# A hybrid decoder step: keys, values and queries by seven block products on pairs of column tiles, with two tensors parked in DRAM

## The chip, the core and the metric

The kernel runs on one core of one Trainium2 chip. The core has a matrix engine (TensorE, in the profile PE, with its weight loads as PEld), a vector engine (VectorE, DVE), a scalar engine (ScalarE, ACT), a third engine for simple element work (GpSimd, POOL) and a sequencer (SyncE, SP) that here only issues DMA transfers. Each engine works through its own list of instructions in order and waits on semaphores. Sixteen DMA engines move data between DRAM and the on-chip memory (SBUF, 128 partitions). Matmul results go to banks of PSUM, an accumulating memory. The metric is the device time of one execution in microseconds (us); lower is better.

## The reference

One layer of a hybrid decoder is computed for 512 prompt tokens and 8 x 4 sample tokens with a width of 2048. One input projection feeds two groups of heads: gated linear attention (GLA), and sparse attention with a compressed branch, a selected branch and a window branch, each with its own keys and values. The parts that matter here:

```python
xn = rmsnorm(h, attn_norm_g[i])
proj = xn @ w_in[i]
gq, gk, gv, gr, ga, nq, kc, vc, ks, vs, kw, vw, ng = jnp.split(proj, offsets, axis=-1)
...
o_gla = rmsnorm(o_gla, gla_norm_g[i]).reshape(B, L, GLA_WIDTH).astype(x.dtype)
o_gla = o_gla * jax.nn.silu(gr)
o_nsa, nsa_new = nsa_mixer(nq, kc, vc, ks, vs, kw, vw, ng, ...)
h = h + jnp.concatenate([o_gla, o_nsa], axis=-1) @ w_out[i]
```

After it come a gated feed-forward part with a short convolution, a per-layer input term and a final norm. `kc` and `vc` (256 columns each) are the keys and values that are compressed; `ks`, `vs`, `kw`, `vw` (256 each) are those of the selected and window branches; `nq` are 8 query heads of 128 columns.

## The kernel before

**Layout.** Everything is kept with features on partitions and tokens along the free dimension. The 544 tokens are two groups `g` of 272 (256 prompt, 16 sample). The 2048 input features are 16 k-tiles. A column tile of `w_in` is 128 output columns. `xn` holds for each k-tile a high and a low part (`xh`, `xl`) of the input times its norm's gain, in the rounded type fp32r; the row scale `R1` is multiplied in after the product.

**One column tile.** `weights` (L155) loads two halves of the tile (512 KB each, 8 k-tiles) through SP into one of three `raw` buffers; ACT casts it to `wh` (L166) and DVE subtracts to get `wl` (L167), three buffers each. `product` (L171) then runs for each of 16 k-tiles three passes (`wh` by `xh`, `wh` by `xl`, `wl` by `xh`) for both token groups: 96 matmuls of 128 x 128 by 272 columns into a two-bank PSUM tile `mp`. DVE evicts with one multiplication by `R1`.

**Order of the stages.** A planner fixes the order of each engine's list when the program is built: it takes operations in the order in which the code states them, and lets a later one go ahead where an earlier one is not ready by its estimate. The stages are: tile 0 (gates), then four GLA heads `h` of 6 tiles each (L463 to L667). At the end of a head the gated outputs are split into high and low parts in `og{h}` (L662 to L665), in the pool `ogla`, and stay there as `o_gla`. Then the loop at L679 makes 12 tiles, two for each of `cmp_k`, `cmp_v`, `slc_k`, `slc_v`, `win_k`, `win_v`. Each is stored by SP (L696); the compression's tiles are reordered by POOL into the tokens `rp` (L699), and values are transposed by PE (L704). The loop at L714 makes 8 query tiles `nq`, which POOL also copies in part into `qs` (L723). Then `xn` is released, and the next stage starts: POOL loads the compression's weights (L353) and the residuals (L735), PE runs the first halves of the output products on `o_gla` (L737, `first_half`) and the compression of the prompt's tokens (`hidden`, L365). Later the attention reuses the `og` buffers for cached keys and values (L831).

**Seven products elsewhere.** The up projection (`up`, L1209) and the down projection (L1366) already multiply pairs with seven block products instead of eight. There `parts` (L1182) splits a half tile of weights and `multiply` (L1189) runs one block product: 8 k-tiles, three passes, one group of tokens, 24 matmuls.

Of the kernel before, what the change touches and what calls it, by code (L numbers as in the profile page):

```python
# [8 lines left out]
F32 = mybir.dt.float32  # L9
F32R = mybir.dt.float32r  # L10
# [93 lines left out]
def trunk(ctx, tc, I, O, stop=None, tap=None):  # L104
# [66 lines left out]
    def product(pp, ws, xs, groups=slice(0, G), ks=None):  # L171
        n = len(ws)
        for k in ks or range(n):
            (wh, wl), (xh, xl) = ws[k], xs[k]
            for w, x, first, last in ((wh, xh, k == 0, False), (wh, xl, False, False), (wl, xh, False, k == n - 1)):
                for g in range(G)[groups]:
                    mm = nc.tensor.matmul(pp[g][:, :GN] if isinstance(pp, list) else pp[:, g, :GN], w, x[:, g],  # L177
                                          start=first, stop=last)
        return mm
# [278 lines left out]
    def blk(t, b):  # L458
        return t[:, b // 2, (b % 2) * 128:(b % 2) * 128 + 128]

    o_gla = []
    ntile = 1
    for h in range(4):  # L463
        qk = []
# [192 lines left out]
        for dv in range(2):  # L657
            f = flat(oT[dv])
            nc.vector.scalar_tensor_tensor(f, f, v1("gn", dv), flat(rs), op0=ALU.mult, op1=ALU.mult)
            nc.vector.tensor_mul(oT[dv], oT[dv], sg[dv])  # L660
            if dv == 0:
                og = op_.tile([128, 2, 2, G, GN], F32R, tag=f"og{h}", name=f"og{h}")  # L662
            hi, lo = og[:, dv, 0], og[:, dv, 1]
            nc.scalar.copy(hi, oT[dv])
            nc.vector.tensor_sub(lo, oT[dv], hi.bitcast(F32))  # L665
# [10 lines left out]
    rp = {}  # L676
    vt = {}
    vn = {}
    for ty, name in enumerate(("cmp_k", "cmp_v", "slc_k", "slc_v", "win_k", "win_v")):  # L679
        keep = name in ("slc_k", "win_k")  # L680
        if name[:3] == "cmp":
            rp[name] = kp.tile([128, 4, 16, 2, 8], F32, name="rp_" + name)
        elif not keep:
            vt[name] = ap.tile([128, 4, 256], F32, name="vt_" + name)
            vn[name] = ap.tile([32, 256], F32, name="vn_" + name)
        for g in range(2):
            pp = main_ps()
            product(pp, weights(wsrc("w_in", ntile)), xn)
            ntile += 1
# [5 lines left out]
            nc.vector.tensor_mul(f, pp[:, :, :GN], R1)  # L695
            nc.sync.dma_start(O[name][g], f)  # L696
            if name[:3] == "cmp":
                for a in range(2):
                    nc.gpsimd.tensor_copy(rp[name][:, 2 * a:2 * a + 2, :, g].rearrange("p c j n -> p c n j"),  # L699
                                          f[:, a, :PN].rearrange("p (c n j) -> p c n j", n=8, j=16))  # L700
            elif not keep:
                s = side_ps()
                for b in range(4):
                    nc.tensor.transpose(s[:, b * 128:b * 128 + 128], blk(f, b), ident)  # L704
                nc.scalar.copy(vt[name][:, :, g * 128:g * 128 + 128], s.rearrange("p (b c) -> p b c", b=4))
                fs = kp.tile([128, 32], F32, tag="fs", bufs=2, name="fs")
# [4 lines left out]
    nq = []  # L711
    qs = ap.tile([128, 2, 8, 32], F32, name="qs")
    nc.gpsimd.memset(qs, 0.0)
    for h in range(8):  # L714
        pp = main_ps()
        product(pp, weights(wsrc("w_in", ntile)), xn)
        ntile += 1
        q = ap.tile([128, G, GN], F32, tag=f"nq{h}", name=f"nq{h}")
        nc.vector.scalar_tensor_tensor(q, pp[:, :, :GN], ATT_SCALE, R1, op0=ALU.mult, op1=ALU.mult)
        nq.append(q)  # L720
        r = h % 4
        for gr in range(2):
            nc.gpsimd.tensor_copy(qs[:, h // 4, 4 * gr:4 * gr + 4, 4 * r:4 * r + 4],  # L723
                                  q[:, gr, PN:].rearrange("p (b t) -> p b t", t=DS))
# [20 lines left out]


    cp, cp_s = pool("cmp", "left")
    ckp = ap.tile([128, 2, 32], F32, name="ckp")
    cvp = ap.tile([128, 2, 128], F32, name="cvp")
# [18 lines left out]
    kp_s.close()  # L768
    tap("ckp", ckp)
    tap("cvp", cvp)  # L770
    if stop == "cmp":
# [15 lines left out]

    attention_out(bp, range(4))
    lp, lp_s = pool("ple", "left")
    OS = ap.tile([128, 8, 32], F32, name="OS")  # L790
# [120 lines left out]
    def sample_step(i):  # L911
# [8 lines left out]
            s_a(*sunits[i])  # L920
        if i == len(sunits):
            tap("OS", OS)

    def split(hi, lo, src):
        nc.scalar.copy(hi, src)  # L925
        nc.vector.tensor_sub(lo, src, hi.bitcast(F32))  # L926

    pcTs = {}
    st = {}
# [176 lines left out]
    def split_scaled(hl, src, scale):  # L1106

        if scale is None:
            split(*hl, src)
            return  # L1110
        nc.scalar.activation(hl[0], src, AF.Copy, scale=scale)  # L1111
        nc.vector.scalar_tensor_tensor(hl[1], src, scale, hl[0].bitcast(F32), op0=ALU.mult, op1=ALU.subtract)

    def stemp(pl, bufs=4):
        return pl.tile([128, GN], F32, tag="st", bufs=bufs, name="st")

    def scaled(out, src, scale, other, op):
        nc.vector.scalar_tensor_tensor(out, src, scale, other, op0=ALU.mult, op1=op)

    first = True  # L1120
    for n in [k + h * HK for k in range(HK) for h in range(2)]:
# [54 lines left out]
    def set_size(name, ph):  # L1176
# [5 lines left out]
    def parts(raw, kn=8, neg=False):  # L1182
        wh = wp.tile([128, 8, 128], F32R, tag="wh", bufs=3, name="wh")
        wl = wp.tile([128, 8, 128], F32R, tag="wl", bufs=3, name="wl")
        w3 = [a[:, :kn].rearrange("p k n -> p (k n)") for a in (raw, wh, wl)]
        split_scaled(w3[1:], w3[0], -1.0 if neg else None)
        return wh, wl

    def multiply(ps, w, a, start, stop):  # L1189
        n = len(a)  # L1190
        for k in range(n):
            for i, (wi, xi) in enumerate(((0, 0), (0, 1), (1, 0))):
                nc.tensor.matmul(ps[:, :GN], w[wi][:, k], a[k][xi], start=start and k == 0 and i == 0,  # L1193
                                 stop=stop and k == n - 1 and i == 2, skip_group_check=True)

    def bank(tag):
        return st_.tile([128, 512], F32, tag=tag, bufs=2, name=tag)
# [458 lines left out]
```

## Time and profile before

| what | us |
|---|---|
| median of 3 timed runs | 2716.22 |
| lowest and highest of them | 2716.19 and 2719.57 |
| the profiled execution | 2723.27 |
| its span, first to last instruction | 2721.4 |
| ACT busy in it | 1150.4 |
| POOL busy in it | 446.1 |

The profile is of one execution. Its page gives each engine's busy time, forty slices of the span, the chain of work that ended last, and groups of equal instructions. The trace behind it answers further views: instructions in order of time (start, duration, engine, line, what is written and read, and in brackets the idle time before and what ended it; an "x2" behind a line says that two instructions are merged in it), tables by stretches of time, who waited for whom, and DMA issues with their time to landing. Matmuls are pipelined: the duration of one is longer than the distance between two starts.

### The profile page before, as it was taken

What the parts mean: (1) busy time and instruction counts of PE and PEld (TensorE: products, weight loads), DVE (VectorE), ACT (ScalarE), POOL (GpSimd) and SP (SyncE); (2) the same over time, 40 slices, a digit from 0 to 9 for tenths busy, and PEclk for the clock granted to TensorE, in tenths of its full rate; (3) what the DMA queues carried; (4) which work ended last, traced back from release to release, by engine and by line L of the source; (5) the groups of instructions that cost most, each with busy time, mean ns of one, the idle gap of its engine ahead of it and who ended that gap; (6) DMA issues with size and microseconds to landing.
All of it is one profiled execution on the core that took longest, in us unless ns stands there. A gap on an engine that the chain in (4) does not pass through costs nothing.

```text
span 2721.4 us, 51097 instructions
## 1 busy us (share of the span) xinstructions
PE 2659.3 (98%) x21258; PEld 2606.8 (96%) x21258; DVE 1770.4 (65%) x2541; ACT 1150.4 (42%) x1811; POOL 446.1 (16%) x591
## 2 busy tenths in 40 slices
PE   8999999999999999999999999999999999999997
PEld 7999999999999779999999999999989999999997
DVE  5333543322256667998888888888887777876434
ACT  4333433221135445554444544444454544544332
POOL 4631101101201210032111211121110111102000
PEclk9999999999999989999999999999999999999998
DMA  6432322332524733333443334333444665746332
GB/s 246 134 109 72 94 95 90 117 106 90 205 71 157 286 108 112 138 124 111 140 133 112 122 121 141 124 111 124 131 177 140 165 171 143 233 116 184 130 111 98
DMA packets 130665, 366.88 MB, mean 135 GB/s; under 512 B 16928, under 2 KB 42512, under 8 KB 127360
## 3 DMA queue, kind: packets, MB, share of 16 engines
q1 hardware_dynamic: 103856, 287.25, 31.3%
q0 software_dynamic: 26576, 76.36, 10.2%
q8 instruction: 167, 2.74, 0.4%
q14 instruction: 66, 0.54, 0.1%
HBM read 298.93 MB, written 64.61 MB: 134 GB/s over the span
## 4 chain that ended last, share of the span: by engine, by line
PE 91%; DVE 3%; issue 3%; DMA 2%; ACT 1%; POOL 0%; SPq 0%; DVEq 0%; POOLq 0%; ACTq 0%
PE mp L177 31%; PE X L1193 26%; PE Y L1193 13%; PE Z L1193 7%; PE mq L177 3%; PE sp L365 3%; PE sp L1002 1%; PE sp L962 1%; DMA xf<-in_xT 1%; DMA ds4l<-dd_s 1%; PE sp L983 1%; PE so L622 1%; PE sp L998 0%; ACT wh L925 0%; PE sp L851 0%
## 5 line engine op out<-in xcount | busy, mean ns | idle before, releaser
L925 ACT CAST wh<-raw 128x1024 fp32r<-128x1024 f32 (+1 forms) x397 | 404.9, 1031 | 495.2 <-PE X L1193 231.5
L926 DVE TENSOR_TENSOR wl<-raw,wh 128x1024 fp32r<-128x1024 f32 (+1 forms) x397 | 471.4, 1196 | 85.5 <-ACT wh L925 85.4
L166 ACT CAST wh<-raw 128x1024 fp32r<-128x1024 f32 (+2 forms) x175 | 171.8, 984 | 457.5 <-PE mp L177 398.3
L167 DVE TENSOR_TENSOR wl<-raw,wh 128x1024 fp32r<-128x1024 f32 (+2 forms) x175 | 200.0, 1145 | 221.4 <-ACT wh L166 218.0
L177 PE MATMUL mp<-xh,wh 128*128 128x272 f32 x1408 | 298.4, 292 | 2.5 <-DVE qk L471 2.5
L177 PE MATMUL mp<-xl,wh 128*128 128x272 f32 x1408 | 299.8, 292 | 0.0
L177 PE MATMUL mp<-xh,wl 128*128 128x272 f32 x1408 | 297.3, 291 | 0.9 <-DVE wl L167 0.9
L177 PEld LDWEIGHTS mp<-xh,wh 128*128 128x128 f32 x1408 | 224.0, 190 | 4.7 <-issue 2.7
L177 PEld LDWEIGHTS mp<-xl,wh 128*128 128x128 f32 x1408 | 224.0, 190 | 1.9 <-issue 0.7
L177 PEld LDWEIGHTS mp<-xh,wl 128*128 128x128 f32 x1408 | 223.3, 190 | 2.3 <-DVE wl L167 1.1
L1254 POOL COPY cvo<-ae 128x2 f32<-128x2 f32 x43 | 52.6, 1223 | 699.7 <-DVE ae L1250 699.7
L1193 PE MATMUL Y<-s,wh 128*128 128x272 f32 x688 | 132.1, 287 | 0.0
L1193 PE MATMUL X<-a,wh 128*128 128x272 f32 x688 | 131.2, 288 | 0.0
L1111 ACT ACTIVATE wh<-raw 128x896 fp32r<-128x896 f32 (+1 forms) x72 | 69.4, 964 | 94.7 <-PE X L1193 48.3
L1193 PEld LDWEIGHTS X<-a,wh 128*128 128x128 f32 x688 | 108.4, 189 | 0.0
L1193 PEld LDWEIGHTS Y<-s,wh 128*128 128x128 f32 x688 | 107.9, 188 | 0.0
L1428 POOL DMA_DIRECT2D rd<-e x48 | 41.7, 868 | 371.3 <-DVE e L1421 327.0
L1193 PE MATMUL X<-s2h,wh 128*128 128x272 f32 x344 | 99.8, 290 | 1.2 <-ACT wh L925 1.2
L1193 PE MATMUL Z<-a12h,wh 128*128 128x272 f32 x344 | 99.9, 290 | 0.4 <-ACT wh L925 0.4
L1193 PE MATMUL X<-a11h,wh 128*128 128x272 f32 x344 | 99.8, 290 | 0.2 <-ACT tt L1242 0.2
L1193 PE MATMUL Y<-s1h,wh 128*128 128x272 f32 x344 | 99.4, 289 | 0.1
L1193 PE MATMUL X<-a11l,wh 128*128 128x272 f32 x344 | 99.4, 289 | 0.0
(528 smaller groups left out, 8104.6 us busy)
## 6 DMA issues: line engine op xcount, KB each, us to landing
raw<-in_w_up SPq DMA_DIRECT2D x172, 512.0 KB, 4.5
raw<-in_w_in SPq DMA_DIRECT2D x89, 512.0 KB, 3.6
raw<-in_w_db SPq DMA_DIRECT2D x48, 448.0 KB, 4.0
raw<-in_w_gate SPq DMA_DIRECT2D x32, 512.0 KB, 3.5
raw<-in_w_da SPq DMA_DIRECT2D x32, 448.0 KB, 3.7
rd<-e POOLq DMA_DIRECT2D x48, 272.0 KB, 4.8
raw<-in_w_out SPq DMA_DIRECT2D x24, 512.0 KB, 3.5
dd_s<-st SPq DMA_DIRECT2D x65, 136.0 KB, 4.9
```

What stands on the lines that cost most here:

```text
L166: nc.scalar.copy(wh[:, :m], raw[:, s:s + m])
L167: nc.vector.tensor_sub(wl[:, :m], raw[:, s:s + m], wh[:, :m].bitcast(F32))
L177: mm = nc.tensor.matmul(pp[g][:, :GN] if isinstance(pp, list) else pp[:, g, :GN], w, x[:, g], start=first, stop=last)
L365: nc.tensor.matmul(at[j // 16], w1[j // 16][:, j % 16], rows[:, :, j % 16], start=j == 0, stop=j == 31, skip_group_check=True)
L622: nc.tensor.matmul(sos[dv][:, b * 4:b * 4 + 4], S0[r // 2][:, r % 2, dv * 128:dv * 128 + 128], smp[:, 1, b * 4:b * 4 + 4], start=False, st ...
L925: nc.scalar.copy(hi, src)
L926: nc.vector.tensor_sub(lo, src, hi.bitcast(F32))
L962: nc.tensor.matmul(s[:, :n0], qv, K[:, 0, :n0], start=True, stop=True)
L1111: nc.scalar.activation(hl[0], src, AF.Copy, scale=scale)
L1193: nc.tensor.matmul(ps[:, :GN], w[wi][:, k], a[k][xi], start=start and k == 0 and i == 0, stop=stop and k == n - 1 and i == 2, skip_group_c ...
L1254: nc.gpsimd.tensor_copy(cvo[:, 0:2], ae[:, 512:514])
L1428: nc.gpsimd.dma_start(rdram[2 * n + j], e[j], accum_op=ALU.add)
```

## The change

The four tiles of the compression's keys and values stay as they are. The other eight key and value tiles and the eight query tiles are made in eight pairs by `pair_product`. With the inputs as blocks (k half, token group) A11, A12 (second k half, first group), A21 (first k half, second group), A22, and four half tiles of weights r11, r12, r21, r22 for the two column tiles, seven products of sums give the four outputs. The sums of inputs S1 = A22 - A21, S2 = -(A11 + S1), S3 = A11 - A21 and S4 are made once, by `sums(k)`, two k-tiles behind each of the four compression tiles; S4 is written into the place of A21 within the first pair (`last_sums`). The weights' sums are made in place in the raw buffers, and `R1` is multiplied in at the end of a pair.

To have room, S1 and S2 take the buffers of the gated outputs. Each `og{h}` is stored to DRAM by SP at the end of its head and loaded back by POOL after the last pair; the tokens `rp` are stored by SP and loaded by POOL in the compression stage. S4's sums and `rp` lie first in buffers that queries take later. `split`, `split_scaled`, `scaled`, `parts` and `multiply` move ahead in the file, unchanged; the pool `kvt` closes before the compression, and a pool `nsa2` holds what is made after it.

```diff
@@ gated linear attention, end of a head
-            o_gla.append((hi, lo))
+        og_dram.append(dram.tile([128, 2, 2, G, GN], F32, name=f"ogd{h}"))
+        nc.sync.dma_start(og_dram[h], og.bitcast(F32))
@@ keys, values, queries
+    s4_ = [ap.tile([128, 4, GN], F32, tag=f"nq{i}", bufs=1, name="s4_") for i in range(2)]
...
+    A_["a11"], A_["a12"] = [[half(k + h, 0) for k in range(HK)] for h in (0, HK)]
+    A_["a22"] = [half(k + HK, 1) for k in range(HK)]
+    for name, pl, tags in (("s1", op_, ("og0", "og1")), ("s2", op_, ("og2", "og3")), ("s3", kp, ("s3a", "s3b"))):
+        A_[name] = []
+        for tag in tags:
+            t = pl.tile([128, HK // 2, 2, GN], F32R, tag=tag, bufs=1, name=name)
+            A_[name] += [[t[:, k, 0], t[:, k, 1]] for k in range(HK // 2)]
...
+    def temp():
+        return kp.tile([128, GN], F32, tag="nt", bufs=3, name="nt")
+
+    def sums(k):
+        x11, x21, x22 = [temp() for _ in range(3)]
+        whole(x21, half(k, 1))
+        whole(x22, A_["a22"][k])
+        nc.vector.tensor_sub(x22, x22, x21)
+        split(*A_["s1"][k], x22)
+        whole(x11, A_["a11"][k])
+        nc.vector.tensor_add(x22, x22, x11)
+        split_scaled(A_["s2"][k], x22, -1.0)
+        s4 = s4_[k // 4][:, k % 4]
+        whole(s4, A_["a12"][k])
+        nc.vector.tensor_sub(s4, x22, s4)
+        nc.vector.tensor_sub(x11, x11, x21)
+        split(*A_["s3"][k], x11)
+
+    def last_sums():
+
+        A_["s4"] = [half(k, 1) for k in range(HK)]
+        for k in range(HK):
+            split(*A_["s4"][k], s4_[k // 4][:, k % 4])
...
+    def pair_raw(src):
+        i = nraw_[0] % 4
+        nraw_[0] += 1
+        raw = (wp if i < 3 else kp).tile([128, 8, 128], F32, tag="raw", bufs=3 if i < 3 else 1, name="raw")
+        nc.sync.dma_start(raw, src)
+        return raw
+
+    def pair_product(n, f0, f1):
+
+        r11, r12, r22, r21 = [pair_raw(I["w_in"][n + j, u]) for j, u in ((0, 0), (1, 0), (1, 1), (0, 1))]
+        pp = main_ps()
+        X, Y, Z = pp[:, 0], pp[:, 1], side_ps()
+        multiply(X, parts(r11), A_["a11"], True, False)
+        nc.scalar.copy(f0[:, 0], X[:, :GN])
+        nc.vector.tensor_add(r11, r11, r12)
+        multiply(Y, parts(r11), A_["s1"], True, False)
+        nc.scalar.activation(f1[:, 1], Y[:, :GN], AF.Copy, scale=-1.0)
+        nc.vector.tensor_add(r11, r11, r22)
+        multiply(X, parts(r11), A_["s2"], False, False)
+        nc.scalar.activation(f1[:, 0], X[:, :GN], AF.Copy, scale=-1.0)
+        multiply(Z, parts(r21), A_["a12"], True, True)
+        nc.vector.tensor_add(r21, r21, r11)
+        nc.vector.tensor_add(f0[:, 0], f0[:, 0], Z[:, :GN])
+        nc.vector.tensor_add(r12, r12, r22)
+        multiply(X, parts(r12), A_["s3"], False, False)
+        scaled(f1[:, 1], X[:, :GN], -1.0, f1[:, 1], ALU.add)
+        if "s4" not in A_:
+            last_sums()
+        multiply(X, parts(r21), A_["a22"], False, True)
+        nc.scalar.copy(f0[:, 1], X[:, :GN])
+        multiply(Y, parts(r22), A_["s4"], False, True)
+        nc.vector.tensor_sub(f1[:, 0], f1[:, 0], Y[:, :GN])
...
-                f = kp.tile([128, G, GN], F32, tag="kvf", bufs=3, name="kvf")
-            nc.vector.tensor_mul(f, pp[:, :, :GN], R1)
+                f = kp.tile([128, G, GN], F32, tag="kvf", bufs=2, name="kvf")
+            fs_.append(f)
+            if cmp:
+                pp = main_ps()
+                product(pp, weights(wsrc("w_in", ntile + g)), xn)
+                nc.vector.tensor_mul(f, pp[:, :, :GN], R1)
+                for k in range(4 * ty + 2 * g, 4 * ty + 2 * g + 2):
+                    sums(k)
+        if not cmp:
+            pair_product(ntile, *fs_)
+            for f in fs_:
+                nc.vector.tensor_mul(f, f, R1)
...
+        if cmp:
+            rp_dram[name] = dram.tile([128, 4, 16, 2, 8], F32, name="rpd_" + name)
+            nc.sync.dma_start(rp_dram[name], rp)
...
     for h in range(8):
-        pp = main_ps()
-        product(pp, weights(wsrc("w_in", ntile)), xn)
...
+        if h % 2 == 0:
+            pair_product(ntile, nq[h], nq[h + 1])
+            ntile += 2
+        q = nq[h]
+        nc.vector.scalar_tensor_tensor(q, q, ATT_SCALE, R1, op0=ALU.mult, op1=ALU.mult)
...
+    kp_s.close()
+    o_gla = []
+    for h in range(4):
+        og = op_.tile([128, 2, 2, G, GN], F32R, tag=f"og{h}", name=f"og{h}")
+        nc.gpsimd.dma_start(og.bitcast(F32), og_dram[h])
+        o_gla += [(og[:, dv, 0], og[:, dv, 1]) for dv in range(2)]
     xp_s.close()
@@ compression of the prompt's tokens
-        hidden(w1, rp[name], 1, hTp.unsqueeze(1))
+        rp = cp.tile([128, 4, 16, 2, 8], F32, tag="rp", bufs=2, name="rp")
+        nc.gpsimd.dma_start(rp, rp_dram[name])
+        hidden(w1, rp, 1, hTp.unsqueeze(1))
```

More of the change, by code (lines that the diff above doesn't have):

```diff
@@ L230, in rms_steps, with split, split_scaled, scaled @@
         yield nc.vector.tensor_copy(fo[:, 128 * full:], pq)
+    def split(hi, lo, src):
+        nc.scalar.copy(hi, src)
+        nc.vector.tensor_sub(lo, src, hi.bitcast(F32))
+    def split_scaled(hl, src, scale):
+        if scale is None:
+            split(*hl, src)
+            return
+        nc.scalar.activation(hl[0], src, AF.Copy, scale=scale)
+        nc.vector.scalar_tensor_tensor(hl[1], src, scale, hl[0].bitcast(F32), op0=ALU.mult, op1=ALU.subtract)
+    def scaled(out, src, scale, other, op):
+        nc.vector.scalar_tensor_tensor(out, src, scale, other, op0=ALU.mult, op1=op)
+    def parts(raw, kn=8, neg=False):
+        wh = wp.tile([128, 8, 128], F32R, tag="wh", bufs=3, name="wh")
+        wl = wp.tile([128, 8, 128], F32R, tag="wl", bufs=3, name="wl")
+        w3 = [a[:, :kn].rearrange("p k n -> p (k n)") for a in (raw, wh, wl)]
+        split_scaled(w3[1:], w3[0], -1.0 if neg else None)
+        return wh, wl
+    def multiply(ps, w, a, start, stop):
+        n = len(a)
+        for k in range(n):
+            for i, (wi, xi) in enumerate(((0, 0), (0, 1), (1, 0))):
+                nc.tensor.matmul(ps[:, :GN], w[wi][:, k], a[k][xi], start=start and k == 0 and i == 0,
+                                 stop=stop and k == n - 1 and i == 2, skip_group_check=True)
     xp, xp_s = pool("xn", "left")
@@ L459, in blk @@
         return t[:, b // 2, (b % 2) * 128:(b % 2) * 128 + 128]
-    o_gla = []
+    og_dram = []
     ntile = 1
@@ L674, in trunk, with half @@
     kp, kp_s = pool("kvt", "right")
+    s4_ = [ap.tile([128, 4, GN], F32, tag=f"nq{i}", bufs=1, name="s4_") for i in range(2)]
     kT = {}
-    rp = {}
+    rp_dram = {}
     vt = {}
     vn = {}
+    A_ = {}
+    def half(k, g):
+        return [x[:, g] for x in xn[k]]
+    A_["a11"], A_["a12"] = [[half(k + h, 0) for k in range(HK)] for h in (0, HK)]
[5 more added lines that the diff above has]
+            A_[name] += [[t[:, k, 0], t[:, k, 1]] for k in range(HK // 2)]
@@ new lines, in whole @@
+    def whole(out, hl):
+        nc.vector.tensor_add(out, hl[0].bitcast(F32), hl[1].bitcast(F32))
+    def temp():
[14 more added lines that the diff above has]
+        split(*A_["s3"][k], x11)
@@ L679, in trunk @@
     for ty, name in enumerate(("cmp_k", "cmp_v", "slc_k", "slc_v", "win_k", "win_v")):
         keep = name in ("slc_k", "win_k")
-        if name[:3] == "cmp":
-            rp[name] = kp.tile([128, 4, 16, 2, 8], F32, name="rp_" + name)
+        cmp = name[:3] == "cmp"
+        if cmp:
+            rp = ap.tile([128, 4, 16, 2, 8], F32, tag=f"nq{2 + ty}", bufs=1, name="rp_" + name)
         elif not keep:
@@ L693, in trunk @@
             else:
-                f = kp.tile([128, G, GN], F32, tag="kvf", bufs=3, name="kvf")
-            nc.vector.tensor_mul(f, pp[:, :, :GN], R1)
+                f = kp.tile([128, G, GN], F32, tag="kvf", bufs=2, name="kvf")
[11 more added lines that the diff above has]
+        ntile += 2
+        for g, f in enumerate(fs_):
             nc.sync.dma_start(O[name][g], f)
-            if name[:3] == "cmp":
+            if cmp:
                 for a in range(2):
-                    nc.gpsimd.tensor_copy(rp[name][:, 2 * a:2 * a + 2, :, g].rearrange("p c j n -> p c n j"),
+                    nc.gpsimd.tensor_copy(rp[:, 2 * a:2 * a + 2, :, g].rearrange("p c j n -> p c n j"),
                                           f[:, a, :PN].rearrange("p (c n j) -> p c n j", n=8, j=16))
@@ L705, in trunk @@
                 nc.scalar.copy(vt[name][:, :, g * 128:g * 128 + 128], s.rearrange("p (b c) -> p b c", b=4))
-                fs = kp.tile([128, 32], F32, tag="fs", bufs=2, name="fs")
+                fs = kp.tile([128, 32], F32, tag="fs", bufs=1, name="fs")
                 nc.gpsimd.tensor_copy(fs.rearrange("p (g n) -> p g n", g=2), f[:, :, PN:])
@@ L710, in trunk @@
                 nc.scalar.copy(vn[name][:, g * 128:g * 128 + 128], s[:32, :128])
-    nq = []
+        if cmp:
+            rp_dram[name] = dram.tile([128, 4, 16, 2, 8], F32, name="rpd_" + name)
+            nc.sync.dma_start(rp_dram[name], rp)
+    nqp = [ap.tile([128, 2, G, GN], F32, tag=f"nq{i}", bufs=1, name=f"nq{i}") for i in range(4)]
+    nq = [nqp[h // 2][:, h % 2] for h in range(8)]
     qs = ap.tile([128, 2, 8, 32], F32, name="qs")
@@ L714, in trunk @@
     for h in range(8):
[L715 to L720, printed above, removed]
+        if h % 2 == 0:
+            pair_product(ntile, nq[h], nq[h + 1])
+            ntile += 2
+        q = nq[h]
+        nc.vector.scalar_tensor_tensor(q, q, ATT_SCALE, R1, op0=ALU.mult, op1=ALU.mult)
         r = h % 4
@@ L747, in trunk @@
     cp, cp_s = pool("cmp", "left")
-    ckp = ap.tile([128, 2, 32], F32, name="ckp")
-    cvp = ap.tile([128, 2, 128], F32, name="cvp")
+    a2, a2_s = pool("nsa2", "right")
+    ckp = a2.tile([128, 2, 32], F32, name="ckp")
+    cvp = a2.tile([128, 2, 128], F32, name="cvp")
     for ci, name in enumerate(("cmp_k", "cmp_v")):
@@ L767, in trunk @@
     cp_s.close()
-    kp_s.close()
     tap("ckp", ckp)
@@ L789, in trunk @@
     lp, lp_s = pool("ple", "left")
-    OS = ap.tile([128, 8, 32], F32, name="OS")
+    OS = a2.tile([128, 8, 32], F32, name="OS")
     oacc = [sa.tile([128, 128], F32, name=f"oacc{p}") for p in range(4)]
@@ L1087, in trunk @@
     more.append(mq)
+    a2_s.close()
     ap_s.close()
@@ L1104, in trunk @@
     rdram = [dram.tile([128, G, GN], F32, name=f"rd{n}") for n in range(KD)]
[L1106 to L1112, printed above, removed]
     def stemp(pl, bufs=4):
         return pl.tile([128, GN], F32, tag="st", bufs=bufs, name="st")
-    def scaled(out, src, scale, other, op):
-        nc.vector.scalar_tensor_tensor(out, src, scale, other, op0=ALU.mult, op1=op)
     first = True
@@ L1180, in trunk @@
              for name in DSETS for ph in range(PHASES)}
[L1182 to L1194, printed above, removed]
     def bank(tag):
```

6 lines of the change are left out of this document (2 added, 4 removed).

## The prediction

> **What bounds the kernel now.** I began with the page: span, busy shares, chain.
>
> ```profile
> span 2721.4 us, 51097 instructions
> PE 2659.3 (98%) x21258; PEld 2606.8 (96%) x21258; DVE 1770.4 (65%) x2541; ACT 1150.4 (42%) x1811; POOL 446.1 (16%) x591
> PE 91%; DVE 3%; issue 3%; DMA 2%; ACT 1%; POOL 0%; SPq 0%; DVEq 0%; POOLq 0%; ACTq 0%
> ```
>
> TensorE (PE) is busy for 98% of the span and owns 91% of the chain that ended last. That is an average, so next I read the table by stretches where the change sits, and the chain in order of time there.
>
> ```profile
> 485.00:515.00 30.00, 30.00 (x241) 30.00 (x240) 8.55 (x8) 5.12 (x6) 6.25 (x6) 1.00 0.40 131
> 515.00:614.00 99.00, 99.00 (x792) 98.96 (x791) 26.18 (x26) 19.77 (x23) 6.04 (x6) 1.00 0.33 108
> 614.00:710.00 96.00, 96.00 (x767) 95.99 (x766) 24.62 (x23) 16.69 (x18) 10.53 (x15) 1.00 0.29 91
> 555.05 12.07 PE mp L177 x96
> 567.67 36.18 PE mp L177 x288
> ```
>
> The columns of the first three rows are the stretch, its length, busy time of PE, weight loads, DVE, ACT and POOL, granted clock, DMA share and GB/s. From 485 to 710 us PE never idles and DVE is about a quarter busy. One column tile is 96 matmuls in 12.06 us, 0.1256 us each: matmuls overlap, so their mean of 290 ns is not their cost; the spacing is. Here time can only come from fewer matmuls.
>
> **The products.** A pair of tiles is now 2 x 96 = 192 matmuls. Seven products of 8 k-tiles and 3 passes are 168. The up projection (L1209) already runs this scheme; its period is read between two equal evictions.
>
> ```profile
> 1494.68 0.39 ACT L1242 COPY tt<-X 128x272 f32<-128x272 f32 x1 [1.16 <-PE X L1193]
> 1515.75 0.39 ACT L1242 COPY tt<-X 128x272 f32<-128x272 f32 x1 [1.15 <-PE X L1193]
> 1473.61:1494.68 21.07, 21.07 (x170) 21.07 (x169) 17.66 (x21) 10.09 (x14) 4.09 (x6) 1.00 0.32 108
> ```
>
> It takes 21.07 us per 168 matmuls, 3.01 per product, with PE full although DVE is busy for 17.66 us. So each pair saves 2 x 12.06 - 21.07 = 3.05 us and eight pairs **24.4 us**.
>
> **DVE inside a pair.** DVE gets 7 splits and 4 sums of weights instead of 4 splits, and ACT 7 casts. DVE's spacing in a dense stretch:
>
> ```profile
> 1110.30 0.43 DVE L926 TENSOR_TENSOR s1l<-st,s1h 128x272 fp32r<-128x272 f32 x1
> 1110.65 0.44 DVE L1112 SCALAR_TENSOR_TENSOR s2l<-st,s2h 128x272 fp32r<-128x272 f32 x1
> 1111.00 0.43 DVE L926 TENSOR_TENSOR s3l<-st,s3h 128x272 fp32r<-128x272 f32 x1
> 1111.36 1.22 DVE L926 TENSOR_TENSOR wl<-raw,wh 128x1024 fp32r<-128x1024 f32 x1
> 1112.49 0.78 DVE L1164 TENSOR_TENSOR st<-s2h,s2l 128x272 f32<-128x272 f32 x2
> ```
>
> A 272-column operation costs 0.35 us and a 1024-column one 1.13. A pair is 11 x 1.13 + 3 x 0.35 + 2 x 0.70 (times R1) = 14.9 of 21.07 us: hidden. The first pair's last_sums adds 8 x 0.35 = 2.8; still hidden. Four raw buffers instead of the eight of the up projection: the next pair's r22 can load once r22's own split is out, some 6.5 us before the pair ends, and the sum that reads it is due about 2.7 us after; loading takes 3.6 (row of the weight loads below): hidden.
>
> **The operand sums are not hidden.** sums(k) has 11 DVE operations of 272 columns. Eight of them are 88 x 0.35 = 30.8 us, and all S1 must stand before the second product of the first pair.
>
> ```profile
> 478.28 0.72 DVE L196 SCALAR_TENSOR_TENSOR rt<-rt,rv 128x544 f32<-128x544 f32 x1 [3.40 <-ACT rt L194]
> 483.60 1.36 DVE L665 TENSOR_TENSOR og<-o,og 128x544 fp32r<-128x544 f32 x2
> 484.99 0.72 DVE L695 TENSOR_TENSOR kvf<-mp,R 128x544 f32<-128x544 f32 x1
> 485.69 1.23 DVE L167 TENSOR_TENSOR wl<-raw,wh 128x1024 fp32r<-128x1024 f32 x1
> 491.72 1.50 DVE L167 TENSOR_TENSOR wl<-raw,wh 128x1024 fp32r<-128x1024 f32 x1
> 491.67 2.04 POOL L699 COPY rp_cmp_k<-kvf 128x256 f32<-128x256 f32 x2 [3.78 <-DVE kvf L695]
> 515.05 0.73 DVE L695 TENSOR_TENSOR kvf<-mp,R 128x544 f32<-128x544 f32 x1 [4.03 <-PE mp L177]
> 1483.84 1.23 DVE L926 TENSOR_TENSOR wl<-raw,wh 128x1024 fp32r<-128x1024 f32 x1 [0.45 <-ACT wh L925]
> ```
>
> The four compression tiles are evicted from 485.0 to 515.05 us; the first pair starts at about 514.6. Sums stand behind the last GLA operation (L665) and the first eviction, since their tiles lie where the GLA pool was. Up to the split of the pair's fifth product DVE owes 30.8 + 4 evictions x 0.70 + 3 splits for the tiles x 1.13 + 9 pair operations x 1.13 + 0.35 = 47.5 us: from 485.0 that ends at 532.5. The fifth product is due at 514.6 + 4 x 3.01 = 526.6. **PE waits 5.9 us** even if DVE never pauses.
>
> Two costs go on top. The split at 491.72 took 1.50 us beside POOL's copies of compression tokens, 0.28 more than alone. POOL has four such stretches, about 8.4 us, so 8.4 x 0.28 / 1.50 = 1.6 us; the bounds are 0 and, if all 47.5 us ran so, 8.9. And each sums hands three values to ACT: 24 waits of between nothing (the dense stretch above) and 0.45 us (row 1483.84), 0 to 10.8. I take 0.5, near the dense stretch, as its mix is the same. Together **8 us**. The lower end is zero, if sums also fill DVE's idle time before 485 (3.40 us before 478.28 alone); the upper end is 5.9 + 1.6 + 10.8 = 18. Were all sums issued ahead of the pair's splits, the first split would end at 485.0 + 30.8 + 2.8 + 3.4 + 1.13 = 523.1, 8.5 us late, some 11 with both extras: inside these bounds.
>
> The Trainium skill, "GPSIMD Engine Reference", section Specifications, says that GpSimd shares its SBUF interfaces with VectorE and contends with DVE instructions with two SBUF inputs. All 11 operations of sums are of that kind, so it speaks against the change; the 1.50 us row agrees, and the page gives no figure. By that rule alone the stall could reach 5.9 + 8.9 + 0.5 = 15 us, by the row it is 8.
>
> **The detour through DRAM.** Each gated output is 128 x 2176 x 4 B = 1.11 MB.
>
> ```profile
> 714.00:716.00 2.00, 2.00 (x18) 2.00 (x17) 0.00 (x0) 0.14 (x1) 2.00 (x5) 1.00 1.03 418
> 716.00:718.00 2.00, 2.00 (x18) 2.00 (x17) 1.06 (x1) 0.91 (x1) 0.59 (x2) 1.00 1.00 410
> 709.76 0.57 PEld L177 LDWEIGHTS mp<-og,wh 128*128 128x128 f32 x4
> 710.87 1.33 POOL L723 COPY qs<-nq 128x16 f32<-128x16 f32 x2 [10.72 <-DVE nq L719]
> 712.15 1.09 POOL L353 DMA_DIRECT2D w<-in_cmp_w  x2
> 718.80 3.68 PE L365 MATMUL sp<-rp_cmp_k,w 128*128 128x64 f32 x32
> out_win_old<-KV SPq DMA_DIRECT2D x8, 1024.0 KB, 5.5
> raw<-in_w_in SPq DMA_DIRECT2D x89, 512.0 KB, 3.6
> ```
>
> The stores of about 5.5 us run on SP's queue amid 12 us tiles at about 110 GB/s: hidden, with up to 2 us if a store waits in front of a weight load. The reloads are 4.46 MB, 11 us at 410 GB/s. S1's memory is free after product 2 of the last pair, 15 us before its end, S2's after product 3, 12 us. If POOL issues them then, they land about 3 us ahead of the first output product, which now starts at 709.76 without a gap: hidden. Cover gone, 12 us (second rival). Then the compression's weights: POOL issues them 2.4 us after the last product, now perhaps 0.5 later for the longer eviction, and 0.5 MB of tokens goes ahead of the residuals, 1.3 us. Two output products (12 us) cover that; before, the token products came at 9. I take **0.5 us**, between 0 and 3.
>
> **Sum.** 24.4 - 8 - 0.5 = 16 us less. The profiled execution took 2723.3 us, 1.9 outside its span, and would take 2707. It lay 7 us above the median of the timed runs, 2716.2; on that the forecast is **2700**, with its own range from 2694 (stall 2) to 2708 (stall 15). About 0.2%, 5.4 us, is what a measurement can tell from no change.
>
> **Rivals.**
> *Sums fully hidden.* DVE's 22 idle us of the 30 from 485, and its idle time before, suffice. For: DVE is a quarter busy. Against: 47.5 us of work for 41.6 us. Then 2692. Chance 0.12.
> *Reloads behind the queue.* POOL's issue order puts the reloads behind the last pair's copies into qs, as it puts the compression's weights now (710.87, then 712.15). They start 2.9 us after the end, take 2 + 11, and the first output product needs the last of them 4.5 us in: PE waits about 12 us, and 2712 results. Against: these buffers rotate in a pool that stays open, while the weights wait for a pool to close. Chance 0.16.
> *Slower: weight loads behind stores.*
>
> ```profile
> SPq L696 <- DVE kvf L695: 32.3, 8, 4.4
> 503.69 0.34 SPq L696 DMA_DIRECT2D out_cmp_v<-kvf  x1
> 505.03 6.35 SPq L152 DMA_DIRECT2D raw<-in_w_in  x2
> ```
>
> SP's queue waits up to 4.4 us for an eviction before a store. If the next pair's four loads stand behind the two stores, each boundary after a key or value pair costs the eviction (0.35 + 0.70 and handing over, about 2), 3.6 for the load, 1.05 for the cast and 1.13 for the split, near 8 us. Four such boundaries are 32 us: 16 slower, 2732. From two boundaries on the gain is gone. Against: the same order now holds without a PE gap, as loads run a tile ahead; for: a pair takes all four raw buffers. Chance 0.09.
>
> The forecast keeps 0.63. Faster by over 0.2%: forecast 0.63, hidden sums 0.12, a few of the second rival, 0.77; within: most of the second, 0.13; slower: the third, and the far end of the second, 0.10. The range is 2691 to 2714: it takes in the first two rivals and leaves out the third.
>
> **What would show it.** Right: 16 pair periods of 21.1 and no 24.1 stretches from the third key tile; a PE gap of 6 to 10 us in the first pair, ended by DVE, with DVE full from 485; no gap at the first output product; reload issues before the last copies into qs. Wrong: gaps at each pair's start ended by a weight split (third rival), a gap at the output product ended by a DMA (second), or stretches in which DVE idles while PE waits, which would mean that order, not DVE's sum, sets the stall.

## The result, and the profile after

| | kernel before | kernel after |
|---|---|---|
| median of 4 runs on one chip, us | 2716.20 | 2748.07 |
| lowest and highest | 2712.73 and 2719.57 | 2741.37 and 2748.28 |
| the profiled execution, us | 2723.27 | 2741.37 |

The ratio is 1.0111, with an interval from 1.0092 to 1.0131. The change costs about 30 us (25 to 36) where I had forecast 16 us less. The two profiled spans differ by only 18.2 us: the profiled execution of before was slower than its median, and that of after was the fastest of its four.

The page of after, the lines that answer to those of before:

```profile
span 2739.6 us, 51068 instructions
PE 2641.8 (96%) x21066; PEld 2586.2 (94%) x21066; DVE 1882.3 (69%) x2717; ACT 1197.7 (44%) x1899; POOL 449.4 (16%) x597
PE 64%; issue 9%; DVE 2%; DMA 2%; POOL 1%; ACT 1%; SPq 0%; DVEq 0%; POOLq 0%; ACTq 0%
```

PE has 192 instructions less, which is the saving that was meant (8 pairs of 24), and is busy for 17.5 us less. But the span is longer: PE now waits. Where it waits is seen in the table by stretches, first of before, then of after (columns as in the prediction: stretch, length, busy PE, weight loads, DVE, ACT, POOL, granted clock, DMA share, GB/s; a clock of 1.00 is TensorE's full clock, 0.50 half of it).

```profile
515.00:562.00 47.00, 47.00 (x377) 46.99 (x376) 12.70 (x12) 8.86 (x10) 3.47 (x3) 1.00 0.34 110
650.00:700.00 50.00, 50.00 (x401) 50.00 (x400) 14.38 (x14) 9.04 (x9) 6.50 (x10) 1.00 0.27 85
727.00:760.00 33.00, 33.00 (x300) 32.84 (x300) 10.43 (x17) 8.98 (x13) 3.41 (x7) 1.00 0.57 203
```

```profile
484.00:515.00 31.00, 31.00 (x249) 31.00 (x249) 29.89 (x59) 10.10 (x19) 5.80 (x6) 1.00 0.48 163
515.00:562.00 47.00, 31.60 (x206) 28.98 (x206) 36.70 (x68) 17.53 (x33) 8.00 (x2) 0.82 0.20 68
650.00:700.00 50.00, 46.31 (x365) 45.44 (x364) 34.85 (x36) 18.73 (x25) 6.33 (x10) 1.00 0.28 85
727.00:760.00 33.00, 27.53 (x157) 27.34 (x157) 5.97 (x7) 4.52 (x6) 13.13 (x26) 0.69 0.90 351
```

A stretch without a gap has 377 matmuls in 47 us; the first pair's stretch (515 to 562) has 206. The pairs behind it lose a little everywhere. And the start of the next stage (727 to 760) has idle time and a granted clock of 0.69. These are three losses, and each has its own cause.

**Every pair.** The pairs' period, read between the copies of the queries into `qs`, and the waits of PE in one of them:

```profile
674.77 1.27 POOL L847 COPY qs<-nq 128x16 f32<-128x16 f32 x2 [14.81 <-DVE nq L844]
698.14 1.27 POOL L847 COPY qs<-nq 128x16 f32<-128x16 f32 x2 [14.81 <-DVE nq L844]
684.96 0.41 PE L259 MATMUL mp<-s,wh 128*128 128x272 f32 x2
688.03 1.04 ACT L234 CAST wh<-raw 128x1024 fp32r<-128x1024 f32 x1 [1.91 <-PE mp L259]
688.99 0.39 ACT L775 ACTIVATE nq<-mp 128x272 f32<-128x272 f32 x1
689.43 0.52 PE L259 MATMUL mp<-s,wh 128*128 128x272 f32 x2 [1.31 <-ACT nq L775]
692.74 0.44 DVE L246 SCALAR_TENSOR_TENSOR nq<-mp,nq 128x272 f32<-128x272 f32 x1 [2.40 <-PE mp L259]
693.23 0.39 PE L259 MATMUL mp<-xh,wh 128*128 128x272 f32 x1 [0.53 <-DVE nq L246]
```

The period is 23.37 us, not 21.07. The third product runs from 684.96 into X, and right behind it the fifth also goes into X: the planner had moved the fourth (into Z, from 681.98) ahead of the third. The fifth must wait until X has been copied out (L775), and on ScalarE that copy stands behind a cast of 1.04 us: PE idles 1.31 us. Then the sixth product, into X again, waits 0.53 us for VectorE's update out of X (L246). With the matmuls that no longer overlap across the two gaps this is 2.30 us per pair; the seven pairs behind the first lose 7 x 2.30 = 16 us.

**The first pair.** PE's rows in the order of time:

```profile
528.44 1.07 PE L259 MATMUL mp<-s,wh 128*128 128x272 f32 x2 [4.79 <-ACT s L234]
532.78 1.07 PE L259 MATMUL mp<-s,wh 128*128 128x272 f32 x2 [3.04 <-ACT s L234]
537.12 1.07 PE L259 MATMUL mp<-s,wh 128*128 128x272 f32 x2 [3.04 <-ACT s L234]
```

The same time in a table of stretches:

```profile
525.00:530.00 5.00, 1.30 (x3) 0.79 (x3) 4.45 (x11) 1.25 (x4) 0.00 (x0) 0.70 0.79 262
530.00:535.00 5.00, 1.30 (x3) 0.79 (x3) 4.80 (x14) 2.24 (x6) 0.00 (x0) 0.50 0.00 0
540.00:545.00 5.00, 4.94 (x24) 4.72 (x24) 1.38 (x3) 0.49 (x3) 0.00 (x0) 0.60 0.27 105
```

VectorE is nearly full from 484 to 541 (29.89 of 31 us in the table above, 4.45 and 4.80 of 5 in the first two rows here), and PE receives the last k-tiles of the operand sums one by one, 4.34 us apart. The clock falls to one half meanwhile. The 171 matmuls that the stretch is short of are 171 x 0.1256 = 21.5 us, of which the waits for evictions in the first pair are 1.35 + 1.31 + 0.53 = 3.2.

**The start of the next stage.** PE's and POOL's rows in the order of time:

```profile
730.38 0.53 POOL L886 DMA_DIRECT2D rp<-rpd_cmp_k  x1
740.38 13.89 PE L395 MATMUL sp<-rp,w 128*128 128x64 f32 x64 [5.47 <-DMA rp<-rpd_cmp_k]
761.12 7.25 PE L395 MATMUL sp<-rp,w 128*128 128x64 f32 x64
```

and the table of short stretches there:

```profile
736.00:738.00 2.00, 0.00 (x0) 0.00 (x0) 1.00 (x1) 0.00 (x0) 0.24 (x1) 1.00 1.04 430
738.00:740.00 2.00, 0.00 (x0) 0.00 (x0) 0.00 (x0) 0.00 (x0) 0.54 (x1) 0.65 0.99 404
745.00:750.00 5.00, 5.00 (x25) 5.00 (x25) 0.00 (x0) 0.00 (x0) 3.49 (x8) 0.50 1.03 390
755.00:760.00 5.00, 5.00 (x28) 5.00 (x27) 0.00 (x0) 1.34 (x3) 0.10 (x1) 0.59 0.85 338
```

The tokens' reload waits for a place in the compression's pool and is issued at 730.38, behind its weights; the DMA engines are full (share 0.99 to 1.04), and it lands 9.9 us later. PE idles 5.47 us. Meanwhile the clock falls to one half, and the 64 token matmuls take 13.89 us where the next 64 take 7.25. That is 5.5 + 6.6 = 12.1 us. The output products behind the tokens keep the low clock too, from 754.02 to about 759.1 (0.59 in the row 755 to 760), which costs half of that time, 2.5 us. Together the loss is **14.6 us**.

**The account.** By these rows: -24.4 (fewer matmuls) + 16.1 (seven pairs) + 21.5 (first pair) + 14.6 (next stage) = 28 us slower, within the measured 25 to 36. The remaining 2 us to the ratio's 30 are not located; the traces of two executions also differ elsewhere, in stages that the change doesn't touch.

### The profile page after: what moved, and what is told of

The parts are those of the page before. It is cut to its first block, busy times and chain, and to the rows that moved or that the text cites. A ratio compares the mean times of both kernels' runs of the same rounds, so it can differ in the third digit from the quotient of the medians.

```text
span 2739.6 us, 51068 instructions
## 1 busy us (share of the span) xinstructions
PE 2641.8 (96%) x21066; PEld 2586.2 (94%) x21066; DVE 1882.3 (69%) x2717; ACT 1197.7 (44%) x1899; POOL 449.4 (16%) x597
## 4 chain that ended last, share of the span: by engine, by line
PE 64%; issue 9%; DVE 2%; DMA 2%; POOL 1%; ACT 1%; SPq 0%; DVEq 0%; POOLq 0%; ACTq 0%
PE X L259 27%; PE Y L259 13%; PE Z L259 7%; PE mp L177 7%; PE mp L259 5%; PE mq L177 3%; DMA KV<-in_cache_slc,idx 1%; PE sp L259 1%; POOL KV L374 1%; PE sp L1130 1%; ACT wh L234 0%; DMA rp<-rpd_cmp_v 0%; DVE resid L1589 0%; DVE wl L235 0%; DMA da22l<-dd_a 0%
## 5 line engine op out<-in xcount | busy, mean ns | idle before, releaser
L234 ACT CAST wh<-raw 128x1024 fp32r<-128x1024 f32 (+1 forms) x453 | 463.6, 1033 | 578.2 <-PE X L259 231.4
L235 DVE TENSOR_TENSOR wl<-raw,wh 128x1024 fp32r<-128x1024 f32 (+1 forms) x453 | 540.4, 1201 | 121.2 <-ACT wh L234 120.3
L177 PE MATMUL mp<-xh,wh 128*128 128x272 f32 x896 | 191.1, 293 | 2.5 <-DVE qk L501 2.5
L177 PE MATMUL mp<-xl,wh 128*128 128x272 f32 x896 | 191.7, 293 | 0.0
L177 PE MATMUL mp<-xh,wl 128*128 128x272 f32 x896 | 190.1, 292 | 0.8 <-DVE wl L167 0.8
L177 PEld LDWEIGHTS mp<-xh,wh 128*128 128x128 f32 x896 | 142.2, 189 | 4.7 <-issue 2.7
L177 PEld LDWEIGHTS mp<-xl,wh 128*128 128x128 f32 x896 | 142.6, 190 | 1.8 <-issue 0.7
L177 PEld LDWEIGHTS mp<-xh,wl 128*128 128x128 f32 x896 | 141.7, 189 | 2.1 <-DVE wl L167 1.1
L259 PE MATMUL mp<-s,wh 128*128 128x272 f32 x384 | 78.0, 300 | 22.7 <-ACT s L234 10.9
L243 DVE SCALAR_TENSOR_TENSOR wl<-raw,wh 128x896 fp32r<-128x896 f32 (+1 forms) x72 | 79.4, 1105 | 29.7 <-ACT wh L242 29.7
```

## The experiments

The chips differ by about 1% (the kernel before took a median of 2719.8, 2745.0 and 2749.3 us on the three that ran these), so the ratio to the kernel before on the same chip is what to compare; the changed kernel stands at 1.0111. Runs e1 to e5 share one chip and e6 to e9 a second, while e10 ran on a third; the changed kernel itself was not run on the second and third, so differences from it are differences of ratios there.

| run | what is different from the changed kernel | median, us | ratio to before | interval |
|---|---|---|---|---|
| e1 | order of products | 2748.79 | 1.0102 | 1.0085 to 1.0119 |
| e2 | compression's pool open early | 2736.17 | 1.0053 | 1.0035 to 1.0071 |
| e3 | one operand sum for all | 2729.40 | 1.0038 | 1.0025 to 1.0051 |
| e5 | e1 and e2 | 2731.77 | 1.0047 | 1.0030 to 1.0064 |
| e6 | own banks for X, Y, Z | 2757.82 | 1.0045 | 1.0029 to 1.0061 |
| e7 | e6 and e2 | 2745.14 | 1.0002 | 0.9987 to 1.0018 |
| e8 | e6, e2 and e3 | 2724.18 | 0.9926 | 0.9900 to 0.9952 |
| e9 | e6, e2, plain products for `slc_k` | 2733.47 | 0.9960 | 0.9947 to 0.9972 |
| e10 | e6, with the changed kernel's order | 2760.43 | 1.0046 | 1.0028 to 1.0064 |

**e1, the order of the products.** My first theory for the pairs was the order alone: third and fifth product follow each other on X. (`multiply` now returns its last matmul, and `tc.issue_after` holds what follows behind it.)

```diff
-        multiply(X, parts(r11), A_["s2"], False, False)
+        third = multiply(X, parts(r11), A_["s2"], False, False)
...
-        multiply(Z, parts(r21), A_["a12"], True, True)
+        w21 = parts(r21)
+        with tc.issue_after(third.ins):
+            multiply(Z, w21, A_["a12"], True, True)
...
+        sixth = multiply(Y, parts(r22), A_["s4"], False, True)
+        nc.vector.tensor_sub(f1[:, 0], f1[:, 0], Y[:, :GN])
+        w21 = parts(r21)
+        with tc.issue_after(sixth.ins):
+            multiply(X, w21, A_["a22"], False, True)
```

> Only the order of the products inside a pair differs from the changed kernel: the fourth product (own bank Z) stands behind the third, and the seventh (bank Y) ahead of the sixth (bank X), so that no two neighbours accumulate in bank X with an eviction between them. Theory 1 (two consecutive products in one bank wait for the eviction between): the period of a pair falls from 23.4 to 21.1 us, the two PE waits of 1.31 and 0.53 us on the evictions vanish, and the time falls by 8 x 2.3 = 18 us, from 2748 to about 2730. Rival (the pair is limited by DVE or by its four raw buffers): the period stays at 23.4 us, the waits move to casts or splits of weights, and the time stays within 4 us of 2748.

The theory fell: 1.0102, and the copies into `qs` are still 23.47 us apart (675.79 to 699.26). The trace of e1 shows what PE now waits for, in the order of time:

```profile
679.33 0.41 PE L259 MATMUL mp<-s,wh 128*128 128x272 f32 x2
683.41 0.39 ACT L773 ACTIVATE nq<-mp 128x272 f32<-128x272 f32 x1
683.85 0.52 PE L259 MATMUL mp<-s,wh 128*128 128x272 f32 x2 [1.36 <-ACT nq L773]
693.20 0.44 DVE L246 SCALAR_TENSOR_TENSOR nq<-mp,nq 128x272 f32<-128x272 f32 x1 [0.79 <-PE mp L259]
693.69 0.39 PE L259 MATMUL mp<-xh,wh 128*128 128x272 f32 x1 [0.53 <-DVE nq L246]
```

L773 of that kernel is the copy out of **Y**, behind the second product (679.33), and it is the third product, into **X**, that waits for it. At 693.69 it is a product into Y that waits for the update out of X. X and Y are the two halves of one tile `mp`. The next theory was therefore that a product waits for evictions of the other half too, so that every order that alternates X and Y keeps the wait.

**e2, the tokens' reload.** The pool of the compression is opened behind `nsa2` on the right side, so that it no longer waits for memory that the pairs hold.

```diff
-    cp, cp_s = pool("cmp", "left")
     a2, a2_s = pool("nsa2", "right")
+    cp, cp_s = pool("cmp", "right")
```

> Only the place of the compression stage's pool differs: it lies on the side that the key and value pool has left, so that its weights and tokens can be loaded before the last pair's products end. Theory 1 (PE stood still at the stage change because the tokens came back 12 us after their issue, and then ran at half clock for some 17 us): the wait of 5.5 us on the tokens and the low clock at 740 to 757 us vanish, and the time falls by 12 to 15 us, to about 2735. Rival (the reload of the gated outputs and the residuals saturate the DMA engines, and these come late whatever is issued first): PE still waits 4 us or more at the stage change, on residuals or output operands, and the time stays within 4 us of 2748.

It came as the first theory said: 1.0053, some 16 us below the changed kernel (12 to 15 were expected). The same stretch in e2:

```profile
727.00:760.00 33.00, 33.00 (x272) 33.00 (x271) 10.57 (x14) 7.92 (x10) 11.15 (x22) 1.00 1.00 394
```

The wait is gone, the clock stays at 1.00, and e2's 64 token matmuls take 7.25 us.

**e3, the operand sums.** Only `sums(0)` is made, and its S1, S2, S3 and S4 stand for all eight k-tiles, so seven eighths of the sums are left out.

```diff
-            split(*A_["s4"][k], s4_[k // 4][:, k % 4])
+            split(*A_["s4"][k], s4_[0][:, 0])
...
-                for k in range(4 * ty + 2 * g, 4 * ty + 2 * g + 2):
-                    sums(k)
+                if ty == g == 0:
+                    sums(0)
+                    for n_ in ("s1", "s2", "s3"):
+                        A_[n_] = [A_[n_][0]] * HK
```

> The operand sums are made for one k-tile alone and used for all eight (77 of the 88 DVE operations of sums are left out, so the pairs' results are not the reference's). Theory 1 (the first pair is late because DVE works through the sums): PE waits in the first pair only for the evictions between products, the clock keeps at 1.0 there, and the time falls by 17 to 21 us, to about 2729. Rival (the first pair is late because of its weights or of the stores in front of them on SP's queue): the stall stays above 10 us and the time within 8 us of 2748.

1.0038, 20 us below the changed kernel. The first pair's stretch in e3:

```profile
515.00:562.00 47.00, 42.20 (x329) 41.12 (x328) 29.27 (x29) 17.10 (x22) 2.05 (x2) 1.00 0.35 119
```

329 matmuls in place of 206: 123 x 0.1256 = 15.4 us come back in this stretch, and the clock stays up. The 48 that are still missing (6.0 us) are mostly waits for evictions in the first two pairs, 3.7 us as the profile lists them, and one of 1.1 us for a weight cast.

**e5, e1 and e2 together.**

> Both the order of e1 and the pool of e2. Theory 1 (the costs are separate and add): 18 + 13 = 31 us less than the changed kernel, about 2717, no slower than before. Rival (the costs cover each other, as one stall hides another): less than 22 us gained, 2726 or more.

1.0047, 17 us below the changed kernel. That is less than the rival's 22, but not for its reason: it is the gain of e2, and no more from the order than the intervals leave room for, as the order alone had gained nothing either.

**e6, banks of their own.**

```diff
-        pp = main_ps()
-        X, Y, Z = pp[:, 0], pp[:, 1], side_ps()
+        X, Y, Z = main_ps()[:, 0], side_ps(), side_ps()
```

> X and Y of a pair are no longer the two halves of one PSUM tile: X is half of one two-bank tile, Y and Z are one-bank tiles, as in the routine for the up matrix; nothing else is edited. The run with the products in order kept the period at 23.4 us, and its waits stood where a product to one half follows the eviction of the other half: the third product waited 1.36 us for the copy of Y, the sixth 0.53 us for the update out of X. Theory A (a wait is set for the whole tile, so each product that follows one on the other half waits for its eviction): both waits go, the period comes to 21.1 to 21.4 us, and eight pairs give back 15 to 18 us: about 2731 us (2727 to 2735). Theory B (the copies themselves are late, queued behind the casts on ScalarE, and hold whatever follows): period 23.3 us, 2746 to 2749 us.

The pairs' period in e6, again between two copies into `qs`:

```profile
670.82:691.83 21.01, 21.01 (x171) 21.01 (x169) 15.53 (x17) 8.50 (x11) 3.03 (x4) 1.00 0.31 101
```

PE is full and the period is 21.0 us, as theory A said; the ratio is 1.0045. But the planner, with separate tiles, also put the fourth product back between third and fifth and the seventh ahead of the sixth. That is the order of e1, so order and banks had changed together.

**e10, own banks in the old order.** The edit of e6, and the order held by waits on the issue, as in e1:

```diff
-        multiply(X, parts(r11), A_["s2"], False, False)
-        nc.scalar.activation(f1[:, 0], X[:, :GN], AF.Copy, scale=-1.0)
-        multiply(Z, parts(r21), A_["a12"], True, True)
+        w3, w21 = parts(r11), parts(r21)
+        fourth = multiply(Z, w21, A_["a12"], True, True)
+        with tc.issue_after(fourth.ins):
+            multiply(X, w3, A_["s2"], False, False)
+        nc.scalar.activation(f1[:, 0], X[:, :GN], AF.Copy, scale=-1.0)
...
-        multiply(X, parts(r21), A_["a22"], False, True)
+        sixth = multiply(X, parts(r21), A_["a22"], False, True)
...
-        multiply(Y, parts(r22), A_["s4"], False, True)
+        w22 = parts(r22)
+        with tc.issue_after(sixth.ins):
+            multiply(Y, w22, A_["s4"], False, True)
```

> In the run with separate banks the planner also put the fourth product back between the third and the fifth, so that banks and order changed together. Here X, Y and Z keep banks of their own, but the products are held in the order that the changed kernel had: first, second, fourth, third, fifth, sixth, seventh, so that third, fifth and sixth follow each other on X. If a wait comes from the evictions of a product's own bank and, where two banks are one tile, from those of the other half too, then third to fifth waits 1.3 us and fifth to sixth 0.5 us again for X alone: period 23.0 to 23.4 us, ratio to the kernel before 1.009 to 1.011, and it takes both, separate banks and the order, to gain the 2.3 us. If separate banks alone are the cure, the period is 21.1 us and the ratio 1.004 to 1.005 in this order too.

The trace of e10 decides it for the pairs; a table of one period, and PE's waits in it:

```profile
664.17:687.59 23.42, 21.58 (x170) 21.14 (x170) 15.89 (x17) 8.51 (x11) 1.60 (x4) 1.00 0.29 91
```

```profile
678.88 0.52 PE L259 MATMUL mp<-s,wh 128*128 128x272 f32 x2 [1.31 <-ACT nq L778]
682.69 0.39 PE L259 MATMUL mp<-xh,wh 128*128 128x272 f32 x1 [0.53 <-DVE nq L246]
```

Both waits are back to the hundredth, now within X (L778 copies X in this kernel). New order with a shared tile: 23.47 us; own banks with the old order: 23.42; both: 21.01. **It takes both.** The total, however, was not what I expected: 1.0046 and not 1.009 to 1.011. Part of the difference is seen in the trace of e10. There all 96 matmuls of the two output products stand behind the last block product, 12 us of cover for the tokens' reload; the changed kernel has run 31 of them ahead of it.

```profile
749.11 12.28 PE L396 MATMUL sp<-rp,w 128*128 128x64 f32 x64 [1.32 <-DMA rp<-rpd_cmp_k]
```

This is (5.47 - 1.32) + (13.89 - 12.28) = 5.8 us less than in the changed kernel, and the low clock behind the tokens lasts 3.4 us in place of 5.1, another 0.8 us. And the stretch from 515 to 562 has 232 matmuls, 26 more: 3.3 us. That makes 10 of some 18 us; the rest stays open. The profiled execution of e10 was among its slowest (2766.95 of 2755.65 to 2767.39), so its trace says little of the total. What the pairs are worth in time is better read from e5 and e7, which both have the early pool and differ in the banks (with the order that the planner makes of them): 1.0047 against 1.0002, 12 us, with some 6 us either way.

**e7, e6 and e2.**

> The banks of e6 and the early pool for the compression of e2 together. If the two losses are independent they add up: 16 plus 12 us below the changed kernel, about 2720 us (2715 to 2724), level with the kernel before. If the pairs' waits only hide the reload (theory B, or a reload that is late again because the pairs end 16 us sooner), it is 2730 us or more.

1.0002: the two gains add up, and the kernel is level with the one before.

**e8, e7 with one operand sum.** As in e3, seven eighths of the sums are left out.

> As e7, and the operand sums are made for one token block only and used for all eight, so that seven eighths of that work are left out and the outputs are not the reference's. All three losses are then gone: 16, 12 and 20 us below the changed kernel, about 2700 us (2695 to 2705), which is the sum that the prediction made without its stall of 8 us (2692 to 2700). If a fourth loss is there, it stays above 2708 us.

0.9926, that is 0.0185 x 2716 = 50 us below the changed kernel and 20 (13 to 27) below the kernel before. The prediction's sum without a stall was 24.4 - 0.5 = 23.9 less than before; so the three losses are nearly all that there was.

**e9, all sums, `slc_k` by plain products.** Its two tiles take 24 us of PE during which the sums can go on.

```diff
-            if cmp:
+            if name in ("cmp_k", "cmp_v", "slc_k"):
                 pp = main_ps()
                 product(pp, weights(wsrc("w_in", ntile + g)), xn)
                 nc.vector.tensor_mul(f, pp[:, :, :GN], R1)
+            if cmp:
...
-        if not cmp:
+        if name not in ("cmp_k", "cmp_v", "slc_k"):
             pair_product(ntile, *fs_)
```

> As e7, with all sums, and the two column tiles of slc_k made by plain products (as those of the compression are), so that seven pairs are left and 24 us more of TensorE work stand beside the sums. It costs the 3 us that one pair saves. If the stall at the first pair is VectorE being full from 484 to 541 us, the 21 us of it shrink to 0 to 5 us: 2702 to 2708 us, faster than both kernels. If the stall comes from the clock or from the order of the first pair alone, it moves to the second pair with its size: 2720 us or more.

0.9960 with an interval from 0.9947 to 0.9972: 11 us faster than the kernel before, and 41 faster than the changed one. The forecast of 2702 to 2708, made for a chip on which the kernel before takes 2716 us, would be 0.995 to 0.997. The stretches up to 562 us and PE's waits from 484 to 745 us in e9:

```profile
484.00:515.00 31.00, 31.00 (x249) 31.00 (x248) 25.49 (x49) 13.81 (x20) 4.14 (x5) 1.00 0.51 173
515.00:562.00 47.00, 47.00 (x377) 47.00 (x376) 43.19 (x82) 20.99 (x38) 4.39 (x4) 1.00 0.31 103
```

```profile
PE sp L890 <- ACT hTp L397: 1.6, 1, 1.6
PE mp L259 <- DVE wl L235: 1.5, 2, 0.7
PE mp L259 <- ACT wh L234: 0.5, 2, 0.3
```

377 matmuls in 47 us: no gap is left where the first pair had lost 21 us in the changed kernel and 17 us in e7 (241 matmuls there), while VectorE does the same sums (43 of 47 us). All that PE waits for up to 745 us is in the last three rows: 1.6 us behind the first tokens, and 2.0 us for weights. The stall did not move on to the second pair, so what made it was VectorE's work that has to be done before the first pair, and not the pair itself. How much of it comes from the place that the planner gave to `last_sums` and the weights' sums is not shown.

## Why the prediction was wrong

- **"Products: each pair saves 3.05 us" failed.** The matmuls went as counted (192 fewer), but the period of 21.07 us was taken from `up`, "which already runs this scheme". The scheme was the same, the PSUM tiles were not: `up` has X, Y and Z in tiles of their own, the pair has X and Y in one. I read the period of a routine and not what it rests on. With the shared tile and the planner's order the period is 23.37 us, and the seven pairs behind the first give back 16 of the 24 us. None of the rivals had a product wait for an eviction from its own PSUM tile.
- **"The operand sums are not hidden" was right in kind, and the stall of 8 us was too small a term.** VectorE was full from 484 us, and the wait ended with the sums, handed over by ScalarE. But 15 (e3's stretch) to 20 us (e3's ratio) came of it, about twice the 8 and near or above my upper end of 18. The sum took VectorE's work up to the fifth product's split as one dense row of 0.35 and 1.13 us operations. In the trace, the last `sums(k)` are 4.34 us apart instead of 11 x 0.35 = 3.85, with short waits for ScalarE's casts in them; the planner put splits of `last_sums` (from 505.34 on) and weight sums of the pair (from 507.38 on) ahead of the last of them; and PE needs a k-tile of every sum in turn, so it idles in steps and its clock falls.
- **"The detour through DRAM: 0.5 us" failed at the tokens**, not at the gated outputs. The bound of 3 us rested on two output products, 12 us, covering the reload; a third of them ran ahead of the last block product. Before the change the tokens were in SBUF and needed no place in the new pool. Now their load is issued 3.8 us after the last product (726.58), into full DMA engines, and lands after 9.9 us, where I had counted 1.3 us for 0.5 MB. It costs 14.6 us; the half clock, more than half of it, was in no term. The cover alone would not have been enough: e10 has all 96 matmuls behind the last block product, and its tokens still came 1.32 us late and ran at half clock.
- **The second rival (reloads behind POOL's queue) fell**, and for the reason that I gave against it. POOL's rows in the order of time, in the kernel after:

```profile
704.31 0.55 POOL L853 DMA_DIRECT2D og<-ogd  x1 [4.90 <-PE mp L259]
711.78 0.53 POOL L853 DMA_DIRECT2D og<-ogd  x1 [0.96 <-PE mp L259]
722.78 0.33 POOL L847 COPY qs<-nq 128x16 f32<-128x16 f32 x2 [7.95 <-DVE nq L844]
```

The first and the last reload of the gated outputs are issued ahead of the last pair's copies into `qs` (722.78 and 728.04), and no product waited for them.
- **The third rival (weight loads behind stores) had the right sign by the wrong mechanism.** Its 2732 is the nearest of the four, but all of PE's waits between 560 and 730 us in the kernel after are on evictions; in e9 all waits for weights together are 2.0 us.
- **VectorE inside a pair** was right: 15.8 us busy in a period, where 14.9 were forecast, and hidden. (There are eight pairs; "16 pair periods" among the signs is a slip.) The Trainium skill ("GPSIMD Engine Reference", section Specifications) spoke against the change by contention of GpSimd with VectorE; the trace agrees that splits beside POOL's copies took up to 1.49 us in place of 1.22. From 484 to 541 us six VectorE rows beside those copies are longer by 1.4 us in all, close to the 1.6 forecast and a small part of the stall.

The Trainium skill has the rule that I passed over: "Perfetto Trace Analysis", section Optimizing Tensor Performance, says that independent groups of matmuls should rotate through different PSUM banks so that the evacuation of one overlaps the matmuls of the next. X and Y were in different banks here, and it did not help while they were one tile: 23.47 us (e1) against 21.01 (e6).

## What to carry to other kernels

A period taken from another routine holds only for its buffers, tiles and order: compare what each product writes, and who must read it before the next may write. Accumulators that are evicted at different times belong in PSUM tiles of their own, in an order that puts other products between two on the same one; here it took both. And when data leaves SBUF for a while, ask of each reload which pool its place comes from and what is in front of it in the queue: here the 4.46 MB that had been worried about were hidden, and 0.5 MB cost 15 us.

## What the runs showed of the clock

The granted clock is a second price of a wait. In the kernel after it fell to one half some 3.7 us into the idle time before 740.38 (the row 738 to 740 above has 0.65). The Trainium skill ("TensorE: Matmul & The Clock Gate", section What's actually happening) names an idle window of about 3.4 us, which agrees. The same section of the Trainium skill states that about 3.4 us of sustained work bring the clock back. The first pair's rows fit that (PE is busy from 539.77, and the clock is back at 544), but the token matmuls do not. They kept PE busy for 13.89 us at a clock of 0.50, and it came back only in the output products behind them, at about 759 us. Nor did every fall need so long a wait: in e10 the token matmuls began at 1.00 after a wait of only 1.32 us, the clock fell some 2 us into them, and they took 12.28 us; in e9 a wait of 1.6 us behind the tokens was followed by a clock of 0.50 from 724 to 727 us. In e2, without a wait, they took 7.25 us at 1.00. Full DMA engines alone do not lower it: in e2 their share was 1.00 as well, and in e10 the clock came back at about 764.5 us with the share still above 1.0. So matmuls of 64 columns kept a high clock without a wait ahead of them, and did not raise a low one; that they are the cause was not tested by itself.
